# A conditioned decoder layer in fp32 on one core: folding of the pool weights, gate, first weight rows and LN powers rearranged

## The chip, the core and the metric

The kernel runs on one core of one Trainium2 chip. The core has TensorE (PE, with its weight loads PEld), VectorE (DVE), ScalarE (ACT), GpSimd (POOL) and SyncE (SP), and 16 DMA engines that move data between device memory and the core. The metric is the time of one execution on the device, in microseconds.

## The reference

A sequence of 4096 tokens with 1024 features goes through one layer: a layer norm that is scaled and shifted by a vector (adaLN), one input projection to 2560 columns, two mixers, one output projection, and a gated residual with a final layer norm.

```python
mod = silu(c) @ w_ada + b_ada                      # c: (1, 1024), w_ada: (1024, 3072)
shift, scale, gate = split(mod, 3)
h = layer_norm(x) * (1 + scale) + shift            # x: (1, 4096, 1024)
u_a, z_a, glu_b, z_b = split(h @ w_in + b_in, ...) # 512, 512, 1024, 512 columns
pooled = causal_multiscale_pool(u_a)               # 4 groups of 128; trailing mean minus token
y_a = (einsum("bsgc,gcd->bsgd", pooled, w_pool) + b_pool) * ls_pool * silu(z_a)
v = glu_b[..., :512] * sigmoid(glu_b[..., 512:])
v = silu(layer_norm(conv31(v) + b_dw) * ln_conv_g + ln_conv_b)
y_b = (v @ w_pw + b_pw) * silu(z_b)
y = concat(y_a, y_b) @ w_out + b_out
out = layer_norm(2 ** 0.25 * x + gate * y) * ln_post_g + ln_post_b
```

## The kernel before

**Products.** A product in fp32 accuracy is made of three matmuls on halves (mm3, L336 to L339): the high half of the weights times the high half of the activations (L337), the same weights times the low half (L338), and the low half of the weights times the high half of the activations (L339). High halves are written by ACT, low halves by DVE as the difference.

**Stages.** The tokens are worked on in 8 blocks (sb) of 512, in three phases over all blocks. In phase 1 a block is normed and modulated, and goes through 8 products of the gated linear unit (columns 8 to 15 of `w_in`, taken in pairs m and 4 + m: `p_<sb>_8` and `p_<sb>_12` are the first pair) and 2 products for z_a or z_b (`p1z`). Its activations x2 (in the rows `x_<sb>_<k>`, k = 0 to 7) are stored to device memory (xD), and its v too (vD). Phase 2 loads x2 again and makes 10 products a block, with pooling on DVE. The convolution runs on DVE (helpers that the rows show as L57x, 31 taps in pairs, on tiles cv, cx and ca), some of it beside phase 1, and its layer norm (conv_ln) lies between the phases' other work. Phase 3 makes the product with w_pw, the output projection and the final norm.

**The start.** The modulation vector is summed on DVE: mod_block (L173 to L192) multiplies eight tiles of w_ada, 128 rows each, by the entries of silu(c), and adds them up (L181), for five blocks of 1, 1, 2, 2 and 2 times 128 columns of scale and shift; a matmul with ones (L186) then sums over the partitions. Block 0's x is turned on TensorE (turn_x) and modulated from there by ACT (L321, L323) and DVE (mod_turned). The weights of phase 1 come as 8 rows of `w_in`, each 128 x 1024 in fp32 (load_row, L389, the tile in the order's rows is `wr`). split_cols cuts each row into high and low halves (L195, `wg0h` to `wg7h` and `wg0l` to `wg7l`), in two pieces: columns 0 to 2 and column 3 of each half of the row (a column here is 128 wide). Six products of block 0 run along with this, row by row; the seventh and eighth, which need column 3, and the z pair, follow when all rows are there.

**Later blocks.** row_stats loads the block's x in four tiles of 128 tokens, and col_stats (L263) takes of each a sum (ACT, L265), a negative mean (DVE), a sum of squares (ACT, L267), a variance (DVE, L268) and a power -0.5 (POOL, L269, one column). to_rows turns the eight columns on TensorE (`xcp`), stores them (rD), and they are loaded again, spread over all partitions (xbc). norm_T loads the transposed x (xk, L291), adds and multiplies (DVE, L292, L294), and mod_xT writes the halves (ACT L303, DVE L304). conv_ln does its statistics with the same col_stats, up to eight tiles a call (`ccp`).

**The fold.** fold_u (L350) multiplies the transposed weights of u_a by w_pool times ls_pool (wpl, made by DVE at L484), so that phase 2 gets the pooled mixer's product in one step. For each of four groups g it loads wT (L352), makes eight matmuls in two banks (L358, `fv`), copies each bank with ACT, stores the result (uD), and makes one matmul for the bias (L363, `bu`). In the code this stands behind block 0. mod_gate (L140) sums the gate's part of w_ada on DVE, and stands behind block 1.

**What sets the order.** The code is written block by block, but a scheduler reorders each engine's instructions by a timeline of its own, within the dependencies. Pools of rotating buffers limit it: 12 for x2, 6 for ca, 2 for cv, 2 for wraw (the raw weights, wT, the fold's result wf and the gate's tiles), 5 for tm (x, xk, xbc), and in PSUM 4 accumulation banks (acc), 2 for turning (tpb) and 2 others (s2b). Nearly all DMAs are issued by SP, in one order; the phase-2 loads of x2 are issued by POOL. The stores of block 0's x2 (L439) carry an explicit dependency on the last modulation sum.

## Time and profile before

| | |
|---|---|
| times of three runs | 1394.03, 1406.85, 1406.32 us (median 1406.32) |
| the profiled execution's own time | 1397.84 us |
| its span | 1395.8 us |
| mean granted clock of TensorE | 0.992 |
| TensorE busy | 97% of the span |
| DVE busy | 86% |
| ACT busy | 31% |
| POOL busy | 9% |
| moved by DMA | 243.81 MB, mean 175 GB/s |

The profile is of one execution, with times counted from the start of its span. In its rows stand the start, the duration or mean duration, the engine, the line of the kernel's text, the operation, and the tiles as out<-in. A bracket at a row's end gives the idle time of that engine just before, and what ended it. An engine runs its instructions in the order in which the program has them, so that one which waits holds up all behind it.

### The profile page before, as it was taken

Reading aid. Unit: us, or ns where it says so; the run is one execution under the profiler, and the core shown is the slowest. Engines: PE = TensorE matmul, PEld = TensorE weight load, DVE = VectorE, ACT = ScalarE, POOL = GpSimd, SP = SyncE. Lnnn points to the kernel's source line nnn. Section 1 sums busy time; section 2 is a strip of 40 time slices with the busy share of each in tenths; the row PEclk is TensorE's granted clock in tenths of the full one; section 3 lists DMA queues with packets and bytes.
Section 4 is the critical chain, followed back from the end, with each engine's and each line's share of the span. In section 5 each row is a group of like instructions: output and inputs, shape, how many; then the busy total and the mean of one; then the engine's idle time right before and its main releaser. Section 6 shows DMA issues by size and latency. Waiting matters only on the chain.

```text
span 1395.8 us, 17137 instructions
## 1 busy us (share of the span) xinstructions
PE 1356.4 (97%) x6045; PEld 1118.5 (80%) x6045; DVE 1193.9 (86%) x2348; ACT 432.6 (31%) x772; POOL 131.0 (9%) x193
## 2 busy tenths in 40 slices
PE   4898999999999999999999999999999999999997
PEld 3777888888888888888888888888888888888886
DVE  8688989983569999899899699999997899998754
...
GB/s 323 328 180 323 214 275 267 163 267 235 180 249 124 226 194 83 131 233 23 182 139 59 234 67 123 131 203 196 157 167 148 139 159 118 162 129 130 186 61 76
DMA packets 113352, 243.81 MB, mean 175 GB/s; under 512 B 15027, under 2 KB 45555, under 8 KB 113267
## 3 DMA queue, kind: packets, MB, share of 16 engines
...
q8 instruction: 47, 0.77, 0.2%
...
## 4 chain that ended last, share of the span: by engine, by line
PE 90%; DMA 5%; DVE 2%; ACT 2%; SPq 1%; issue 1%; DVEq 0%; ACTq 0%
PE po L713 25%; PE p L338 6%; PE p L339 6%; PE p L337 6%; PE p2z L338 4%; PE p2u L338 4%; PE p2z L337 4%; PE p2z L339 4%; PE p2u L337 4%; PE p2u L339 4%; PE pw L689 2%; PE pw L691 2%; PE pw L690 2%; PE p2b L338 2%; PE p2b L337 2%; PE p2b L339 2%
## 5 line engine op out<-in xcount | busy, mean ns | idle before, releaser
L576 DVE SCALAR_TENSOR_TENSOR cx<-cv,wdw,cx 128x513 f32<-128x513 f32 (+1 forms) x240 | 145.7, 613 | 0.7
L576 DVE SCALAR_TENSOR_TENSOR ca<-cx,wsum,ca 128x256 f32<-128x256 f32 (+1 forms) x240 | 143.7, 611 | 0.1
L576 DVE SCALAR_TENSOR_TENSOR ca<-cv,wdw,ca 128x256 f32<-128x256 f32 (+1 forms) x224 | 134.3, 611 | 0.0
L742 POOL TENSOR_TENSOR ors<-ove,mhalf 128x1 f32<-128x1 f32 x32 | 46.9, 1467 | 408.8 <-DVE ove L738 400.4
L736 ACT ACTIVATE ojk<-r,osm 128x1024 bf16<-128x1024 f32 x31 | 35.6, 1148 | 148.3 <-DVE osm L733 148.3
L332 POOL DMA_DIRECT2D x2r<-xD x64 | 34.8, 544 | 402.8 <-PE p2b L339 276.7
L731 DVE SCALAR_TENSOR_TENSOR r<-po,r 128x512 f32<-128x512 f32 x62 | 40.9, 687 | 22.0 <-PE po L713 21.9
L576 DVE SCALAR_TENSOR_TENSOR lx<-lv,wdw,lx 128x257 f32<-128x257 f32 x120 | 57.5, 479 | 0.0
L576 DVE SCALAR_TENSOR_TENSOR la<-lx,wsum,la 128x256 f32<-128x256 f32 x120 | 57.3, 478 | 0.0
L576 DVE SCALAR_TENSOR_TENSOR la<-lv,wdw,la 128x256 f32<-128x256 f32 x112 | 53.3, 478 | 0.0
L269 POOL TENSOR_TENSOR xcs<-smx,mhalf 128x1 f32<-128x1 f32 x28 | 20.7, 740 | 343.9 <-DVE smx L268 343.6
L517 ACT ACTIVATE sz<-p2z,cols 128x512 f32<-128x512 f32 x32 | 22.0, 688 | 95.6 <-PE p2z L339 95.5
L292 DVE TENSOR_TENSOR xk<-xk,xbc 128x1024 f32<-128x1024 f32 x28 | 34.1, 1222 | 17.2 <-DMA xk<-in_x_t_dram 17.2
L303 ACT ACTIVATE x<-xk,shc 128x512 fp32r<-128x512 f32 x56 | 38.0, 719 | 31.5 <-DVE xk L294 31.5
L304 DVE SCALAR_TENSOR_TENSOR x<-xk,shc,x 128x512 fp32r<-128x512 f32 x56 | 40.4, 749 | 8.3 <-ACT x L303 8.3
L524 ACT ACTIVATE u<-p2u,bu 128x512 f32<-128x512 f32 x32 | 22.0, 689 | 70.4 <-PE p2u L339 70.4
L745 DVE SCALAR_TENSOR_TENSOR r<-r,ors,b_bc 128x1024 f32<-128x1024 f32 (+1 forms) x33 | 41.1, 1248 | 3.2 <-POOL ors L742 3.1
L443 ACT ACTIVATE sg<-p,cols 128x512 f32<-128x512 f32 x32 | 21.9, 686 | 70.3 <-PE p L339 69.8
L265 ACT ACTIVATE x<-x 128x1024 f32<-128x1024 f32 x28 | 29.6, 1059 | 40.6 <-DMA x<-in_x_dram 39.7
L713 PE MATMUL po<-wo0h,ya 128*128 128x512 f32 x128 | 41.2, 392 | 0.0
L713 PE MATMUL po<-wo1h,ya 128*128 128x512 f32 x128 | 41.1, 390 | 0.0
L705 DVE SCALAR_TENSOR_TENSOR r<-r,gbo 128x1024 f32<-128x1024 f32 x32 | 39.0, 1218 | 1.7 <-DMA r<-in_x_dram 1.7
...
## 6 DMA issues: line engine op xcount, KB each, us to landing
...
```

Of the source, the lines that this page charges most:

```text
L303: nc.scalar.activation(h2[:, 0, :], z, AF.Identity, bias=shc[:, k : k + 1])
L304: nc.vector.scalar_tensor_tensor(h2[:, 1, :], z, shc[:, k : k + 1], h2[:, 0, :].bitcast(F32), op0=ALU.add, op1=ALU.subtract)
L337: nc.tensor.matmul(ps, w[0], X[0], start=first, stop=False)
L338: nc.tensor.matmul(ps, w[0], X[1], start=False, stop=False)
L339: nc.tensor.matmul(ps, w[1], X[0], start=False, stop=last)
L576: nc.vector.scalar_tensor_tensor(dst, src, wt, dst, op0=ALU.mult, op1=ALU.add)
L705: xg = nc.vector.scalar_tensor_tensor(r, r, ALPHA, gbo, op0=ALU.mult, op1=ALU.add)
L713: mm = nc.tensor.matmul(po[h], lhs, Wo[k][wi][:, h * 512 : (h + 1) * 512], start=(k == 0 and wi == 0 and lhs is yh), stop=last)
L731: nc.vector.scalar_tensor_tensor(r[:, sl], po[h], 1.0, r[:, sl], op0=ALU.mult, op1=ALU.add, accum_out=sm[:, h : h + 1])
L736: nc.scalar.activation(jk, r, AF.Square, bias=sm[:, 2:3], accum_out=ss)
L742: nc.gpsimd.tensor_tensor(rs, ve, mhalf[:, 0:1], op=ALU.pow)
L745: nc.vector.scalar_tensor_tensor(r[:, sl], r[:, sl], rs, b_bc[:, sl], op0=ALU.mult, op1=ALU.add)
```

## The change

Six things are changed.

1. *The fold.* Its four groups go to the ends of blocks 2, 3, 4 and 5. wT of a group is loaded a block earlier, its result wf has a tm buffer, and its banks are those for turning. wpl stands behind block 1 in the code.
2. *The gate.* mod_gate and its two matmuls go into phase 2, behind its third block (GATE_SB = 2).
3. *The first weight rows.* Each row is loaded with 768 of its 1024 columns (columns 0 to 2 of both halves). The remaining column 3 of both halves is loaded afterwards, by eight small loads in two tiles (`w3r`). The raw z weights (wzr) move from wraw to the buffers of gate and gbo.
4. *x of block 1.* Its four tiles are loaded among the first loads, into the ca buffers (x_early), and block 0's stores of x2 come behind the loads of xk for block 1.
5. *The modulation sums.* DVE sums six of the eight tiles; the last two are multiplied on TensorE, which adds them in the same accumulation: per column 3 matmuls in place of 1.
6. *The LN powers.* col_stats scales x by -1/n as it sums, so that the sum is the negative mean, and takes the scale back with -n ahead of the square; the two DVE steps per tile are gone. inv_root adds and takes the power on POOL once per block, on 4 or 8 columns together, and the constant left over goes into s1n and lcg.

The new lines of mod_block, of the statistics and of the fold, and the places where they are called (its other hunks are names and shapes):

```diff
-        for kt in range(KT):
+        nv = KT - 2
+        for kt in range(nv):
...
-                nc.tensor.matmul(ps[:, nk * i + j : nk * i + j + 1], acc[:, 1 - i, j * P : (j + 1) * P],
-                                 ones[:, 0:1], start=True, stop=True)
+                o = ps[:, nk * i + j : nk * i + j + 1]
+                sl = slice(j * P, (j + 1) * P)
+                nc.tensor.matmul(o, acc[:, 1 - i, sl], ones[:, 0:1], start=True, stop=False)
+                for kt in range(nv, KT):
+                    nc.tensor.matmul(o, wts[kt][:, 1 - i, sl], sc[:, kt : kt + 1], start=False, stop=kt == KT - 1)
...
-    def col_stats(src, n, nmean, rstd, name):
-        sm = st.tile([P, 3], F32, tag="sm", bufs=4, name=f"sm{name}")
-        nc.scalar.activation(src, src, AF.Identity, accum_out=sm[:, 0:1])
-        nc.vector.tensor_scalar(nmean, sm[:, 0:1], -1.0 / n, None, op0=ALU.mult)
-        nc.scalar.activation(src, src, AF.Square, bias=nmean, accum_out=sm[:, 1:2])
-        nc.vector.tensor_scalar(sm[:, 2:3], sm[:, 1:2], 1.0 / n, EPS, op0=ALU.mult, op1=ALU.add)
-        nc.gpsimd.tensor_tensor(rstd, sm[:, 2:3], mhalf[:, 0:1], op=ALU.pow)
+    def col_stats(src, n, nmean, ss):
+        nc.scalar.activation(src, src, AF.Identity, scale=-1.0 / n, accum_out=nmean)
+        nc.scalar.activation(src, src, AF.Square, bias=nmean, scale=-float(n), accum_out=ss)
+
+    def inv_root(ss, n):
+        nc.gpsimd.tensor_scalar(ss, ss, n * EPS, None, op0=ALU.add)
+        nc.gpsimd.tensor_tensor(ss, ss, mhalf[:, : ss.shape[1]], op=ALU.pow)
...
-            xt = load_x(i)
-            col_stats(xt, D, cs[:, t : t + 1], cs[:, 4 + t : 5 + t], f"x{i}")
+            xt = x_early[t] if sb == 1 else load_x(i)
+            col_stats(xt, D, cs[:, t : t + 1], cs[:, 4 + t : 5 + t])
+        inv_root(cs[:, 4:8], D)
...
-    def fold_u(g, wpl):
-        wT = wraw(f"wT{g}")
-        nc.sync.dma_start(wT, w_in_t[g * P : (g + 1) * P, :])
-        wf = wraw(f"wf{g}")
+    wTs = []
+
+    def fold_u(g, wpl, wT):
+        wf = ph.tile([P, D], F32, tag="tm", bufs=5, name=f"wf{g}")
...
-            pb = s2_bank(f"fv{g}_{hb}")
+            pb = tp_bank(f"fv{g}_{hb}")
...
-                   cst.tile([P, D], F32, tag=("gate", "gbo")[home - 2], name=f"wr{k}"))
-        nc.sync.dma_start(rows[k], w_in[k * P : (k + 1) * P, 8 * P : 16 * P])
+                   cst.tile([P, D], F32, tag=("gate", "gbo")[home - 2], name=f"wr{k}"))[:, : 6 * P].rearrange(
+                       "p (h c) -> p h c", h=2)
+        nc.sync.dma_start(rows[k], w_in[k * P : (k + 1) * P, 8 * P : 16 * P].rearrange(
+            "p (h c) -> p h c", h=2)[:, :, : 3 * P])
...
+    x_early = []
+    for t in range(TT):
+        xt = s2.tile([P, D], F32, tag="ca", bufs=6, name=f"x{TT + t}", padded_shape=[P, 2 * (HQ + T + 1)])
+        nc.sync.dma_start(xt, tok(xv, TT + t))
+        x_early.append(xt)
...
+        hi, lo = (both(t)[:, :, : 3 * P] for t in Wg[k])
+        nc.scalar.copy(hi, rows[k])
         xT.append(mod_turned(pb, k))
-        split_cols(k, 0, 3)
-        split_cols(k, 3, 4)
+        nc.vector.tensor_tensor(lo, rows[k], hi.bitcast(F32), op=ALU.subtract)
...
+    for q in range(2):
+        raw = wraw(f"w3r{q}").rearrange("p (k h c) -> p k h c", k=4, h=2)
+        for k in range(4):
+            nc.sync.dma_start(raw[:, k], both(w_in[(4 * q + k) * P : (4 * q + k + 1) * P, 8 * P : 16 * P])[:, :, 3 * P :])
+        for k in range(4):
+            hi, lo = (both(t)[:, :, 3 * P :] for t in Wg[4 * q + k])
+            split(hi, lo, raw[:, k])
...
+    nc.vector.tensor_scalar(s1n, s1, math.sqrt(D), None, op0=ALU.mult)
+    lcg = cst.tile([P, MC], F32, name="lcg")
+    nc.vector.tensor_scalar(lcg, vec("lncg", 0, MC), math.sqrt(DH), None, op0=ALU.mult)
...
+        if sb == 0:
+            for k in range(KT):
+                for i in range(2):
+                    after(nc.sync.dma_start(xD[k][0][:, i, :], xT[k][i].bitcast(F32)), x_loads[1])
...
-        if sb == 0:
+        if sb == 1:
...
-            for g in range(MC):
-                fold_u(g, wpl)
-        if sb == 1:
-            mod_gate(gbo)
...
+        if 1 <= sb <= MC:
+            wT = wraw(f"wT{sb - 1}")
+            nc.sync.dma_start(wT, w_in_t[(sb - 1) * P : sb * P, :])
+        if 2 <= sb <= MC + 1:
+            fold_u(sb - 2, wpl, wTs.pop(0))
+        if 1 <= sb <= MC:
+            wTs.append(wT)
...
+        if sb == GATE_SB:
+            mod_gate(gbo)
+            gb = wraw("gb")
+            nc.sync.dma_start(gb, b_ada[2 * D : 3 * D].partition_broadcast(P))
+            for h in range(2):
+                sl = slice(h * 512, (h + 1) * 512)
+                gp = tp_bank(f"gp{h}")
+                nc.tensor.matmul(gp, ones, gbo[:, sl], start=True, stop=True)
...
-            col_stats(pb, DH, cs[:, q : q + 1], cs[:, nq + q : nq + q + 1], f"c{s0}_{q}")
+            col_stats(pb, DH, cs[:, q : q + 1], cs[:, nq + q : nq + q + 1])
+        inv_root(cs[:, nq : 2 * nq], DH)
```

In the whole program TensorE has 5975 rows in place of 5946, DVE 2081 in place of 2223, POOL 139 in place of 173, SP 544 in place of 545, and ACT 625 as before.

On TensorE, at the end of block 0 and the start of block 1, the order of before is this (`fv` and `bu` are the fold's, `x_1_0` the first activations of block 1, `wg0h` and `wg0l` the halves of the first weight row; a number behind a name is the tile's):

```order
L358 MATMUL fv_1_1075<-wpl,wT_1066 128x128 x4
L363 MATMUL bu_1082<-cols,wpl 128x1
L337 MATMUL p_1_8_1192<-x_1_0_962,wg0h 128x512
L337 MATMUL p_1_12_1193<-x_1_0_962,wg0h 128x512
L337 MATMUL p_1_9_1247<-x_1_0_962,wg0h 128x512
L337 MATMUL p_1_13_1248<-x_1_0_962,wg0h 128x512
L358 MATMUL fv_0_1088<-wpl,wT_1085 128x128 x4
L358 MATMUL fv_1_1094<-wpl,wT_1085 128x128 x4
L363 MATMUL bu_1101<-cols,wpl 128x1
L358 MATMUL fv_0_1107<-wpl,wT_1104 128x128 x4
L358 MATMUL fv_1_1113<-wpl,wT_1104 128x128 x4
L338 MATMUL p_1_8_1192<-x_1_0_962,wg0h 128x512
```

In the changed order the same place, from the last matmul of block 0 on, reads:

```order
L348 MATMUL p1z_1_1038<-x_0_7_759,wz1l 128x512
L346 MATMUL p_1_8_1118<-x_1_0_968,wg0h 128x512
L346 MATMUL p_1_12_1119<-x_1_0_968,wg0h 128x512
L346 MATMUL p_1_9_1173<-x_1_0_968,wg0h 128x512
L346 MATMUL p_1_13_1174<-x_1_0_968,wg0h 128x512
L347 MATMUL p_1_8_1118<-x_1_0_968,wg0h 128x512
L348 MATMUL p_1_8_1118<-x_1_0_968,wg0l 128x512
L347 MATMUL p_1_12_1119<-x_1_0_968,wg0h 128x512
L348 MATMUL p_1_12_1119<-x_1_0_968,wg0l 128x512
```

The fold's eight rows are gone from here; the first of them now stand behind the last product of block 2. The first product of block 1 with the low half (L347, which was L338) stands fifth behind block 0's last matmul, where it was thirteenth (one row of the fold precedes the rows shown of before).

On ACT, in the start, the casts of the fifth to eighth weight row and the steps of x_0_4 stand like this before (`x_843` is a tile of block 1's x, whose statistics are L265 and L267; `hs_4` is a step of x_0_4):

```order
L195 CAST wg4h<-wr_409 128x2x384
L195 CAST wg4h<-wr_409 128x2x128
L195 CAST wg5h<-wr_411 128x2x384
L195 CAST wg5h<-wr_411 128x2x128
L265 ACTIVATE x_843,smx_845<-x_843 128x1024
L195 CAST wg6h<-wr_421 128x2x384
L195 CAST wg6h<-wr_421 128x2x128
L321 ACTIVATE x_0_4_628<-xt_4_605,shc,s_281 128x512
L267 ACTIVATE x_843,smx_845<-x_843,xcs_842 128x1024
L195 CAST wg7h<-wr_423 128x2x384
L195 CAST wg7h<-wr_423 128x2x128
L323 ACTIVATE hs_4_630<-x_0_4_628,shn 128x512
```

And in the changed order (L270 and L271 are now the statistics, on the four tiles x_426 to x_432; L430 the cast of 768 columns, and L200 that of column 3):

```order
L430 CAST wg5h<-wr_412 128x2x384
L330 ACTIVATE x_0_4_646<-xt_4_622,shc,s_281 128x512
L270 ACTIVATE x_428,xcs_870<-x_428 128x1024
L332 ACTIVATE hs_4_648<-x_0_4_646,shn 128x512
L270 ACTIVATE x_430,xcs_870<-x_430 128x1024
L271 ACTIVATE x_428,xcs_870<-x_428,xcs_870 128x1024
L430 CAST wg6h<-wr_422 128x2x384
L271 ACTIVATE x_430,xcs_870<-x_430,xcs_870 128x1024
L430 CAST wg7h<-wr_424 128x2x384
L270 ACTIVATE x_432,xcs_870<-x_432 128x1024
L200 CAST wg0h<-w3r_783 128x2x128
L330 ACTIVATE x_0_5_676<-xt_5_652,shc,s_281 128x512
```

The sums of all four tiles of block 1 and the squares of three have moved ahead of x_0_5's first step, and so has a cast of column 3, while the second cast of each weight row is gone from its place; the other seven casts of column 3 and the last square follow ahead of x_0_5's second step.

On SP, the DMA issues around the load of wpl are these before (`cv` is the convolution's load of v, `rD` and `xbc` are the store of block 1's statistics and their load):

```order
L482 DMA wpl<-in_w_pool_dram 128x4x128
L439 DMA xD_0_157<-x_0_7_741 128x512
L446 DMA vD_0_165<-v_0_894 128x512
L565 DMA cv_0_6444<-vD_0_165 128x2x256
L446 DMA vD_0_173<-v_1_899 128x512
L446 DMA vD_0_181<-v_2_904 128x512
L565 DMA cv_1_6501<-vD_0_173 128x2x256
L276 DMA rD_270<-rowsx_877 8x128
L286 DMA xbc_880<-rD_270 128x1024
L291 DMA xk_0_882<-in_x_t_dram 128x2x512
L291 DMA xk_2_887<-in_x_t_dram 128x2x512
L291 DMA xk_4_978<-in_x_t_dram 128x2x512
```

And in the changed order:

```order
L510 DMA wpl<-in_w_pool_dram 128x4x128
L516 DMA wT_1798<-in_w_in_t_dram 128x1024
L467 DMA vD_0_165<-v_0_900 128x512
L467 DMA vD_0_173<-v_1_905 128x512
L282 DMA rD_270<-rowsx_883 8x128
L598 DMA cv_0_6382<-vD_0_165 128x2x256
L598 DMA cv_1_6439<-vD_0_173 128x2x256
L293 DMA xbc_886<-rD_270 128x1024
L300 DMA xk_0_888<-in_x_t_dram 128x2x512
L300 DMA xk_2_893<-in_x_t_dram 128x2x512
L467 DMA vD_0_181<-v_2_910 128x512
L300 DMA xk_4_984<-in_x_t_dram 128x2x512
```

The stores of block 0's x2 (xD_0) are gone from here, and stand behind the last load of xk. wpl and two loads of wT stand ahead of the store of v and of the statistics.

More of the change, by code (lines that the diff above doesn't have):

```diff
@@ L34 @@
 EARLY = 2
+GATE_SB = 2
 PERSB = (1, 1, 1, 1, 1, 1, 0, 0)
@@ L66, in tile_layer @@
     nc.vector.memset(ones, 1.0)
-    mhalf = cst.tile([P, 4], F32, name="mhalf")
+    mhalf = cst.tile([P, 2 * TT], F32, name="mhalf")
     nc.vector.memset(mhalf, -0.5)
@@ L391, in load_row, with both @@
         rows[k] = (wraw(f"wr{k}") if home < 2 else
-                   cst.tile([P, D], F32, tag=("gate", "gbo")[home - 2], name=f"wr{k}"))
-        nc.sync.dma_start(rows[k], w_in[k * P : (k + 1) * P, 8 * P : 16 * P])
+                   cst.tile([P, D], F32, tag=("gate", "gbo")[home - 2], name=f"wr{k}"))[:, : 6 * P].rearrange(
+                       "p (h c) -> p h c", h=2)
+        nc.sync.dma_start(rows[k], w_in[k * P : (k + 1) * P, 8 * P : 16 * P].rearrange(
+            "p (h c) -> p h c", h=2)[:, :, : 3 * P])
+    def both(t):
+        return t.rearrange("p (h c) -> p h c", h=2)
     mods = ((0, 1), (1, 1), (2, 2), (4, 2), (6, 2))
@@ L400, in tile_layer @@
             load_row(k)
-    def split_cols(k, m0, m1):
-        split(*(t.rearrange("p (h c) -> p h c", h=2)[:, :, m0 * P : m1 * P] for t in (*Wg[k], rows[k])))
+    x_early = []
[3 more added lines that the diff above has]
+        x_early.append(xt)
     xT = []
@@ L424, in tile_layer @@
     for q in range(2):
-        raw = wraw(f"wzr{q}")
+        raw = cst.tile([P, D], F32, tag=("gate", "gbo")[q], name=f"wzr{q}")
         nc.sync.dma_start(raw.rearrange("p (k n) -> p k n", k=4),
@@ L436, in tile_layer @@
     gbo = cst.tile([P, D], F32, tag="gbo", name="gbo")
-    for k in range(KT):
-        for i in range(2):
-            after(nc.sync.dma_start(xD[k][0][:, i, :], xT[k][i].bitcast(F32)), last, True)
     def glu(sb, m, pa, pg):
@@ L485, in tile_layer @@
             nc.vector.tensor_tensor(bpl, vec("b_pool", 0, 4), vec("ls", 0, 4), op=ALU.mult)
-            for g in range(MC):
-                fold_u(g, wpl)
-        if sb == 1:
-            mod_gate(gbo)
-            gb = wraw("gb")
-            nc.sync.dma_start(gb, b_ada[2 * D : 3 * D].partition_broadcast(P))
-            for h in range(2):
-                sl = slice(h * 512, (h + 1) * 512)
-                gp = tp_bank(f"gp{h}")
-                nc.tensor.matmul(gp, ones, gbo[:, sl], start=True, stop=True)
-                nc.vector.tensor_tensor(gate_bc[:, sl], gp, gb[:, sl], op=ALU.add)
-            nc.sync.dma_start(gbo, b_out.partition_broadcast(P))
-            nc.vector.tensor_tensor(gbo, gbo, gate_bc, op=ALU.mult)
+        if 1 <= sb <= MC:
[5 more added lines that the diff above has]
+            wTs.append(wT)
     ph_ctx.close()
@@ L554, in tile_layer @@
             nc.sync.dma_start(zD[1][sb][:, m - 2, :], sz)
+        if sb == GATE_SB:
[6 more added lines that the diff above has]
+                nc.tensor.matmul(gp, ones, gbo[:, sl], start=True, stop=True)
+                nc.vector.tensor_tensor(gate_bc[:, sl], gp, gb[:, sl], op=ALU.add)
+            nc.sync.dma_start(gbo, b_out.partition_broadcast(P))
+            nc.vector.tensor_tensor(gbo, gbo, gate_bc, op=ALU.mult)
     ph_ctx.close()
```

10 lines of the change are left out of this document (6 added, 4 removed).

## The prediction

> **What bounds the kernel now.** I read the page first, then the table of engines by stretch, then TensorE in order of time where that table shows it short of work.
>
> ```profile
> PE 1356.4 (97%) x6045; PEld 1118.5 (80%) x6045; DVE 1193.9 (86%) x2348; ACT 432.6 (31%) x772; POOL 131.0 (9%) x193
> ...
> 0.00:35.00 35.00, 14.86 (x57) 11.77 (x58) 28.16 (x75) 13.93 (x19) 4.16 (x37) 0.97 1.00 323
> 35.00:70.00 35.00, 30.96 (x150) 25.13 (x149) 21.09 (x45) 19.20 (x31) 1.10 (x2) 0.98 0.97 328
> 70.00:105.00 35.00, 31.65 (x145) 26.33 (x144) 31.09 (x70) 15.07 (x28) 1.62 (x2) 0.90 0.55 178
> 105.00:140.00 35.00, 31.58 (x144) 26.95 (x145) 29.77 (x77) 16.23 (x29) 2.89 (x4) 0.90 0.88 322
> ...
> 560.00:700.00 140.00, 140.00 (x634) 115.96 (x633) 129.09 (x220) 28.78 (x70) 15.54 (x24) 1.00 0.40 137
> ```
>
> The columns are the stretch, its length, then busy time of PE, PEld, DVE, ACT and POOL, the granted clock, the DMA share and GB/s. TensorE bounds the kernel: of the 39.4 us in which it is idle, 20.1 + 4.0 + 3.4 + 3.4 lie in the first 140 us, and in 560 to 700 it has none. So only what happens before 140 us can shorten the program; work that leaves DVE, ACT or POOL later is worth nothing by itself. Within those 140 us there is one hole, at 95 to 115:
>
> ```profile
> 95.00:100.00 5.00, 2.72 (x11) 1.75 (x10) 5.00 (x9) 2.21 (x5) 0.00 (x0) 0.75 0.84 239
> 100.00:105.00 5.00, 3.93 (x18) 3.85 (x18) 5.00 (x11) 3.17 (x7) 0.00 (x0) 0.56 0.14 30
> 105.00:110.00 5.00, 1.58 (x7) 1.61 (x8) 5.00 (x11) 0.63 (x2) 0.00 (x0) 0.78 0.87 314
> 110.00:115.00 5.00, 5.00 (x19) 4.37 (x18) 4.72 (x10) 3.27 (x5) 0.00 (x0) 0.54 0.91 280
> ...
> 80.42 0.27 PE L73 MATMUL xcp<-ident,xcs 128*8 128x128 f32 x1
> ...
> 93.50 1.95 PE L358 MATMUL fv<-wpl,wT 128*128 128x128 f32 x16
> ...
> 97.62 2.07 PE L337 MATMUL p<-x,wg0h 128*128 128x512 f32 x4 [2.01 <-ACT x L303]
> 99.96 3.75 PE L358 MATMUL fv<-wpl,wT 128*128 128x128 f32 x16 [0.27 <-DMA wT<-in_w_in_t_dram]
> ...
> 108.42 3.76 PE L358 MATMUL fv<-wpl,wT 128*128 128x128 f32 x16 [4.49 <-DMA wT<-in_w_in_t_dram]
> 111.83 0.77 PE L338 MATMUL p<-x,wg0h 128*128 128x512 f32 x1
> ```
>
> TensorE works in order. It finishes block 0 at 93.50, and the second matmul of block 1 (L338) starts only at 111.83: three folds stand before it, two of them waited for a load, and the granted clock fell to about half, so a fold that took 1.95 us takes 3.75.
>
> **The change, part by part.** *The fold.* All four folds leave this place. L338 of block 1 then waits for the later of two things: TensorE's end of block 0, and the low half of x_1_0 from DVE. The latter was written here:
>
> ```profile
> 72.59 0.69 DVE L484 TENSOR_TENSOR wpl<-wpl,lsb 128x512 f32<-128x512 f32 x1
> ...
> 77.48 0.44 DVE L570 TENSOR_TENSOR cx<-cv 128x271 f32<-128x271 f32 x1 [1.62 <-DMA cv<-vD]
> ...
> 78.11 0.34 DVE L574 TENSOR_SCALAR ca<-cv,wdw 128x256 f32<-128x256 f32 x1
> 78.37 0.35 DVE L574 TENSOR_SCALAR ca<-cx,wsum 128x256 f32<-128x256 f32 x1
> ...
> 79.03 0.48 DVE L576 SCALAR_TENSOR_TENSOR ca<-cv,wdw,ca 128x256 f32<-128x256 f32 x1
> 79.42 0.48 DVE L576 SCALAR_TENSOR_TENSOR ca<-cx,wsum,ca 128x256 f32<-128x256 f32 x1
> ...
> 94.91 1.23 DVE L292 TENSOR_TENSOR xk<-xk,xbc 128x1024 f32<-128x1024 f32 x1
> 96.05 1.42 DVE L294 SCALAR_TENSOR_TENSOR xk<-xk,s,xbc 128x512 f32<-128x512 f32 x2
> 97.37 0.49 DVE L576 SCALAR_TENSOR_TENSOR ca<-cv,wdw,ca 128x256 f32<-128x256 f32 x1
> ...
> 103.93 0.76 DVE L304 SCALAR_TENSOR_TENSOR x<-xk,shc,x 128x512 fp32r<-128x512 f32 x1
> ...
> 67.30 0.38 SPq L482 DMA_DIRECT2D wpl<-in_w_pool_dram  x1
> ...
> 82.62 2.06 SPq L291 DMA_DIRECT2D xk<-in_x_t_dram  x4
> ```
>
> From start to start a tap costs 0.39 us, a first tap 0.26, an L292 1.14, a pair of L294 1.32. In the changed order 2 sums (0.36 each), 6 first taps, 21 taps, 4 of L292, 2 pairs of L294 and one L445 (0.67) stand from the first conv instruction to that low half, and its own 0.7 ends it: 0.7 + 1.6 + 8.2 + 4.6 + 2.6 + 0.7 + 0.7 = 19.1 us. The transposed sums (xcp) stand about 10 us earlier, ahead of p_0_11, but SP issues their store behind the wpl load, the second wT load (which waits for wpl's product on DVE, 5.3 us after wpl's issue) and two stores of v. Block 0 starts its tail about 1.4 us earlier (below), so wpl goes at 66, its product at 71.3, xk's loads at about 76 instead of 82.62, and the first conv instruction at about 77 as before. I take 77 + 19.1 = 96.1 for L338. If the loads come in time and DVE is not late the bound is TensorE itself, 92.1; if the start loses what I expect it to gain, and a load is late, 100.
>
> L338 is thus 111.83 - 96.1 = 15.7 us earlier. Three folds must still be paid, warm, at the 1.95 us of the row at 93.50 and a little for bu: -6.1. Behind 111.83 the matmuls ran at a clock of 0.54 for the 3.2 us to 115, which gives +1.6. Net 11.2 us, from 7 (at 100) to 15 (at 92.1). The folds in blocks 2 to 5 have wT loaded a block ahead, so their loads are covered; ACT empties their banks while the second half is multiplied. (A block has 240 matmuls; at 634 in 140 us that is 53 us.) The 16 stores of x_0 now wait on SP until the last xk load has landed, and behind them stand the stores of v, z and x_1 and the loads of block 2's x; these are wanted a block later, so I count 0, and a microsecond for a microsecond should they come late.
>
> *The modulation sums.* They take 16 sums off DVE and put 32 matmuls of one column on TensorE.
>
> ```profile
> L181 DVE SCALAR_TENSOR_TENSOR macc<-wa,sc,macc 128x512 f32<-128x512 f32 x21 | 15.3, 747 | 0.1
> L181 DVE SCALAR_TENSOR_TENSOR macc<-wa,sc,macc 128x256 f32<-128x256 f32 x14 | 6.8, 483 | 0.3
> ...
> 43.68 0.95 PE L186 MATMUL mod<-ones,macc 128*128 128x1 f32 x8
> 44.48 0.63 PE L73 MATMUL xt<-ident,x 128*128 128x128 f32 x4
> ```
>
> Off DVE go 6 x 0.75 and 4 x 0.48 (two per block of modulation): 6.4 us of DVE time, ahead of which TensorE waited. Eight records, four matmuls, take 0.80 us, so 32 more cost 6.4 us of TensorE, in a stretch where it is idle 24 us. By these rows the two sums cancel only where TensorE waits for nothing else; I count the lead as 0 for the first weight row, where the mod matmuls run cold and now stand ahead of all of its products, and as some 3 us by the fourth.
>
> *Weight rows and the early x.* Rows of 768 columns save 8 x 128 KB, but three of the four loads of x for block 1 now come ahead of the last rows, so these land as before. What they add is ACT work just there:
>
> ```profile
> 41.42 1.14 ACT L195 CAST wg4h<-wr 128x768 fp32r<-128x768 f32 x2 [1.48 <-DMA wr<-in_w_in_dram]
> ...
> 47.04 1.06 ACT L265 ACTIVATE x<-x 128x1024 f32<-128x1024 f32 x1 [2.94 <-DMA x<-in_x_dram]
> 48.00 0.19 ACT L265 ACTIVATION_READ_ACCUMULATOR x<-x 128x1 f32 x1
> ...
> 50.02 1.14 ACT L267 ACTIVATE x<-x,xcs 128x1024 f32<-128x1024 f32 x1
> 51.06 0.19 ACT L267 ACTIVATION_READ_ACCUMULATOR x<-x,xcs 128x1 f32 x1
> ...
> 59.50 0.48 PE L338 MATMUL p<-x,wg5h 128*128 128x512 f32 x1
> ```
>
> ACT has four statistics (2.4 us each, 9.5), four casts of 768 and eight of 256 (0.7 and 0.3 each, the pair at 41.42 split by its columns), and the three steps of x_0_4 and x_0_5 (2.2, at two thirds of the L267 row's 1.14 for half its columns) in a row from about 40, where the first early x lands (1.4 us ahead of the row at 41.42): 17.1 us. The last of them ends at 57, and the low half of x_0_5 is there at about 58.4 after one DVE step, where the old one let L338 start at 59.50. The 3 us of lead thus shrink to 1 to 1.5; bounds +3 and -5 by when the eight small loads of columns 3 land. This is inside the 96.1.
>
> *The rest.* The gate's ten or so DVE microseconds go to phase 2, where DVE has 10.9 us of slack in 140 and the result is needed only in phase 3: 0. The powers and 120 single-column DVE steps lie beside TensorE: 0, as long as xcp and ccp are not late (third rival). The final tail is untouched.
>
> [...]
>
> **The rivals.** (1) *No hole at all*: DVE and loads keep up, L338 at 92 or the start gains its 3 us: 15 to 18 us, 1397.84 - 16.5 = 1381. For it: the xk loads meet less traffic, since the 16 stores of x_0 now wait for them. Against: the taps ahead of x_1_0. (2) *The start pays*: ACT's queue and the w3 loads hold x_0_5 for 4 us more than the old order did, and block 1 slips with it: 11.2 - 5 = 6 us, 1392. For it: DVE has all eight low halves of columns 3 and both of wz ahead of x_0_5 and x_0_6. (3) *Slower: the powers on POOL.*
>
> ```profile
> L269 POOL TENSOR_TENSOR ccs<-smc,mhalf 128x1 f32<-128x1 f32 x32 | 24.3, 767 | 95.6 <-DVE smc L268 95.0
> L269 POOL TENSOR_TENSOR xcs<-smx,mhalf 128x1 f32<-128x1 f32 x28 | 20.7, 740 | 343.9 <-DVE smx L268 343.6
> ```
>
> No row shows a power of 4 or 8 columns. Should it cost by the column, 4 x 0.74 and 8 x 0.77 come after the last sum where one came: +2.2 and +5.4 us, plus the added sum (0.7). TensorE would stand at xcp and ccp wherever they were placed for less: if none of this is covered, 7 x 2.9 + 4 x 2.9 + 2 x 6.1 = 44 us, 1431; it turns the sign from about a quarter of it on. The other bound is a cost by the instruction, where nothing is late. I take the latter, since ACT had to wait for xcp on TensorE and not the reverse, so there is slack. [...] (4) *Nothing moves*: the folds meet new waits in their blocks worth what they cost here.
>
> **How the numbers follow.** The forecast against the profiled execution: 1397.84 - 11.2 = 1386.6. That execution lies low among the four that are known (1394.03, 1397.84, 1406.32, 1406.85); their middle is 1402.1, the stated median 1406.32 (8.5 over the profiled one), and nothing in the profile says which level the changed kernel meets. So 1402.1 - 11.2 = 1391, and I take 1390. Chances: forecast 0.55, no hole 0.15, the start pays 0.17, powers 0.07, nothing 0.06. Low end: 1394 less 16.5, 1377; high end: 1406 less 5, 1402; both ends of the unknown terms and three of the other cases fall inside. A difference of 1% (14 us) is about what a measurement of this kernel tells from none; faster by that means under 1392.3. The forecast does it in six of ten, no hole in nine of ten, the start in two of ten: 0.33 + 0.13 + 0.03 = 0.49. Slower by 1% comes only from the powers and a little of the rest, 0.07.
>
> **What would show it.** L347 of block 1 (the old L338) at 94 to 98 us, at full clock or nearly; no idle before the folds' matmuls; TensorE idle 2 to 5 us between 48 and 60; nothing idle behind 120; ACT without a pause from 40 to 57. Wrong if block 1 starts behind 100, if xcp or ccp get a wait for POOL, or if gp waits for DVE.

## The result, and the profile after

The changed kernel takes 1420.96 us (median of four runs, 1417.60 to 1421.26), against 1401.23 us before (four runs, 1394.03 to 1406.85): ratio 1.0129, 95% interval 1.0083 to 1.0176. The kernel before took 1393 to 1400 us in some executions and 1403 to 1409 in others, for a reason that no run shows, and the share of the longer ones differs between the batches of the experiments (6 of 19, 0 of 14, 15 of 21 and 2 of 19), so that a ratio can shift by up to 0.7% on that account alone. The changed kernel is slower by 1.3%, where 1390 was forecast. The profiled execution has a span of 1419.4 us, against 1395.8 before.

The first row of the changed kernel's page, and its table of engines by stretch (stretch, length, busy time of PE, PEld, DVE, ACT and POOL, granted clock, DMA share, GB/s):

```profile
PE 1371.0 (97%) x6109; PEld 1129.2 (80%) x6109; DVE 1178.4 (83%) x2220; ACT 432.5 (30%) x772; POOL 115.5 (8%) x159
...
35.00:70.00 35.00, 35.00 (x175) 29.48 (x174) 18.30 (x40) 23.25 (x40) 1.27 (x2) 0.90 0.72 228
70.00:105.00 35.00, 31.49 (x127) 25.07 (x126) 28.91 (x59) 10.88 (x16) 0.00 (x0) 0.90 0.90 311
105.00:140.00 35.00, 35.00 (x156) 28.89 (x155) 31.31 (x73) 12.95 (x21) 1.58 (x2) 1.00 0.65 243
140.00:280.00 140.00, 133.91 (x606) 110.25 (x606) 124.98 (x233) 59.24 (x99) 14.24 (x6) 0.98 0.54 194
280.00:420.00 140.00, 140.00 (x639) 116.06 (x638) 50.68 (x68) 57.16 (x94) 3.79 (x6) 1.00 0.59 212
...
840.00:980.00 140.00, 126.88 (x551) 102.86 (x550) 138.16 (x296) 36.16 (x67) 4.40 (x7) 0.94 0.45 151
980.00:1120.00 140.00, 137.61 (x604) 112.36 (x603) 126.36 (x256) 49.02 (x90) 14.13 (x11) 0.99 0.45 154
```

The hole of the first 140 us has closed as forecast, but TensorE is now idle 6.1 us in 140 to 280 and 13.1 us in 840 to 980, where before it was not idle at all. Its waits, grouped (us in all, times, longest), name the places:

```profile
PE mod L190 <- DVE macc L183: 10.0, 2, 8.9
PE po L747 <- ACT ya L200: 9.1, 2, 8.6
PE ccp L74 <- POOL ccs L275: 6.1, 2, 4.5
...
PE pw L723 <- ACT vp L200: 2.3, 1, 2.3
...
PE xcp L74 <- POOL xcs L275: 1.6, 1, 1.6
```

How far the changed kernel is behind (+) the kernel before, by the silu that follows each block's last z product (phase 1), by the last of phase 2, and at the end of the span:

| end of | before | after | difference |
|---|---|---|---|
| block 0 | 93.70 | 96.81 | +3.1 |
| block 1 | 170.04 | 155.49 | -14.6 |
| block 2 | 226.37 | 210.53 | -15.8 |
| block 3 | 284.30 | 277.45 | -6.9 |
| block 6 | 447.45 | 447.63 | +0.2 |
| phase 2 | 946.70 | 947.67 | +1.0 |
| program | 1395.8 | 1419.4 | +23.6 |

Block 0's +3.1 is not TensorE's: its last matmul of that block starts at 93.51 where it started at 93.26, but the silu stands on ACT behind a step that waits for DVE. So a lead of 16 us was won at the start, given back in blocks 3 to 6, and another 22.6 us were lost in phase 3. Three places have to be read.

**Block 1.** TensorE's timeline, as the prediction asked for it:

```profile
97.53 0.63 PE L346 MATMUL p<-x,wg0h 128*128 128x512 f32 x1 [2.96 <-ACT sgz L479]
98.72 0.80 PE L347 MATMUL p<-x,wg0h 128*128 128x512 f32 x1 [0.55 <-DVE x L313]
```

L347 starts at 98.72, where L338 started at 111.83. The wait of 2.96 us ahead of it ended, by the profile, with the silu of block 0's last z product (`sgz`, at 96.81), which stood on ACT behind a step of block 1's x that had waited for DVE.

**Block 3.** The timeline of POOL, then of DVE, then of TensorE:

```profile
233.52 4.50 POOL L274 TENSOR_SCALAR xcs<-xcs 128x4 f32<-128x4 f32 x1 [60.34 <-ACT x L271]
238.11 1.04 POOL L275 TENSOR_TENSOR xcs<-xcs,mhalf 128x4 f32<-128x4 f32 x1
239.13 6.19 POOL L274 TENSOR_SCALAR ccs<-ccs 128x4 f32<-128x4 f32 x1
...
300.31 0.23 POOL L274 TENSOR_SCALAR xcs<-xcs 128x4 f32<-128x4 f32 x1 [53.88 <-ACT x L271]
...
237.86 0.75 DVE L466 SCALAR_TENSOR_TENSOR v<-p,cols,sg 128x512 f32<-128x512 f32 x1
...
244.48 0.75 DVE L609 SCALAR_TENSOR_TENSOR ca<-cx,wsum,ca 128x512 f32<-128x512 f32 x1
246.94 1.23 DVE L301 TENSOR_TENSOR xk<-xk,xbc 128x1024 f32<-128x1024 f32 x1 [1.71 <-DMA xk<-in_x_t_dram]
...
239.20 0.27 PE L74 MATMUL xcp<-ident,xcs 128*8 128x128 f32 x1 [1.58 <-POOL xcs L275]
246.49 0.38 PE L74 MATMUL ccp<-ident,ccs 128*8 128x128 f32 x1 [4.50 <-POOL ccs L275]
```

An addition on four columns, 0.23 us at 300, takes 4.50 and 6.19 us here. The first ends when DVE begins an instruction that reads v's product from PSUM (237.86), the second when DVE has nothing to do (244.48 + 0.75 = 245.23); until then DVE ran one tap behind the other. TensorE waits for both, and its next matmuls, to 251, are 0.43 us apart at a granted clock of 0.50, where they were 0.23 us apart at 240.

**The start of phase 3.** TensorE, and DVE's L640, the step with which a convolution norm begins:

```profile
953.40 0.38 PE L74 MATMUL ccp<-ident,ccs 128*8 128x128 f32 x1 [1.64 <-POOL ccs L275]
...
964.93 1.22 PE L747 MATMUL po<-wo0h,ya 128*128 128x512 f32 x2 [8.62 <-ACT ya L200]
...
421.88 2.49 DVE L640 TENSOR_TENSOR ca<-ca,cbc 128x512 f32<-128x512 f32 x4 [0.26 <-DMA cbc<-cD]
630.03 4.63 DVE L640 TENSOR_TENSOR ca<-ca,cbc 128x1024 f32<-128x1024 f32 x4 [0.47 <-DMA cbc<-cD]
...
958.43 2.50 DVE L640 TENSOR_TENSOR ca<-ca,cbc 128x512 f32<-128x512 f32 x4 [0.36 <-DMA cbc<-cD]
```

And the same steps of the kernel before:

```profile
400.08 2.50 DVE L606 TENSOR_TENSOR ca<-ca,cbc 128x512 f32<-128x512 f32 x4 [8.56 <-DMA cbc<-cD]
596.17 4.63 DVE L606 TENSOR_TENSOR ca<-ca,cbc 128x1024 f32<-128x1024 f32 x4 [3.64 <-DMA cbc<-cD]
...
918.96 2.49 DVE L606 TENSOR_TENSOR ca<-ca,cbc 128x512 f32<-128x512 f32 x4
```

The last norm of the convolution's main part came 27.7 us ahead of the end of phase 2, and now comes 10.8 us behind it, in the middle of the first work of phase 3. TensorE's 8.62 us hang on it by a buffer. The spread rows of the norm (`cbc`) and phase 3's load of the pooled mixer's result (`ya`) share one more pool, of two buffers (tag `bc` in the code), so the load of ya goes out when L640 has ended, at 958.43 + 2.50 = 960.93, and ACT and TensorE wait for it. The changed kernel's two rows, then the load in the kernel before, behind its own L606 (918.96 + 2.49 = 921.45) but 30.5 us ahead of the first matmul that uses it (952.02):

```profile
960.95 0.32 SPq L710 DMA_DIRECT2D ya<-yD  x1
964.26 1.14 ACT L200 CAST ya<-ya 128x512 fp32r<-128x512 f32 x2 [2.53 <-DMA ya<-yD]
...
921.48 0.32 SPq L676 DMA_DIRECT2D ya<-yD  x1
```

In e1 and e13 the load goes out within 0.04 us of L640's end as well (927.79 and 939.31). The lateness, 39.5 us at this norm, builds up earlier: it was 21.8 us at the first norm, and 33.9 at the second. Why the first is late is seen in the changed kernel's SP and ACT:

```profile
391.94 2.28 SPq L266 DMA_DIRECT2D x<-in_x_dram  x3
394.32 0.38 SPq L370 DMA_DIRECT2D uD<-wf  x1
394.74 1.42 SPq L266 DMA_DIRECT2D x<-in_x_dram  x1
...
412.98 0.26 ACT L281 COPY rowsx<-xcp 8x128 f32<-8x128 f32 x1 [3.31 <-PE xcp L74]
413.14 0.25 ACT L281 COPY rowsc<-ccp 8x128 f32<-8x128 f32 x1
```

The x of block 7 is loaded at 392 to 396, around the store of the last fold's result wf, where the kernel before loaded it at 356 to 365. Its statistics come with it, and the rows of the first convolution norm (`rowsc`) stand behind the rows of block 7 (`rowsx`) on ACT, although TensorE had turned them at 246.49. DVE cannot go on with the convolution before that norm has released its buffers, so it has 50.68 us of work in 280 to 420 where it had 79.16.

### The profile page after: what moved, and what is told of

It reads as the page before. It is cut to its first block, busy times and chain, and to the rows that moved or that the text cites. A ratio compares the mean times of both kernels' runs of the same rounds, so it can differ in the third digit from the quotient of the medians.

```text
span 1419.4 us, 17051 instructions
## 1 busy us (share of the span) xinstructions
PE 1371.0 (97%) x6109; PEld 1129.2 (80%) x6109; DVE 1178.4 (83%) x2220; ACT 432.5 (30%) x772; POOL 115.5 (8%) x159
## 4 chain that ended last, share of the span: by engine, by line
PE 88%; DVE 5%; DMA 3%; ACT 1%; POOL 1%; SPq 1%; issue 1%; DVEq 0%; ACTq 0%; POOLq 0%
PE po L747 24%; PE p L346 7%; PE p L347 7%; PE p L348 7%; PE p2u L347 4%; PE p2z L347 4%; PE p2z L348 4%; PE p2u L348 4%; PE p2u L346 4%; PE p2z L346 4%; PE p2b L348 2%; PE p2b L347 2%; PE p2b L346 2%; PE pw L723 2%; PE pw L725 2%; PE pw L724 2%
## 5 line engine op out<-in xcount | busy, mean ns | idle before, releaser
L609 DVE SCALAR_TENSOR_TENSOR cx<-cv,wdw,cx 128x257 f32<-128x257 f32 (+1 forms) x240 | 145.0, 611 | 1.2
L466 DVE SCALAR_TENSOR_TENSOR v<-p,cols,sg 128x512 f32<-128x512 f32 x32 | 23.8, 745 | 71.9 <-ACT sg L464 68.9
L539 ACT ACTIVATE sz<-p2z,cols 128x512 f32<-128x512 f32 x32 | 22.0, 688 | 121.8 <-PE p2z L348 113.1
L301 DVE TENSOR_TENSOR xk<-xk,xbc 128x1024 f32<-128x1024 f32 x28 | 34.1, 1218 | 21.8 <-DMA xk<-in_x_t_dram 17.7
L200 ACT CAST yb<-z 128x512 fp32r<-128x512 f32 x32 | 19.8, 617 | 81.1 <-DVE z L730 66.4
L747 PE MATMUL po<-wo2h,ya 128*128 128x512 f32 x128 | 40.0, 390 | 0.4 <-ACT ya L200 0.4
```

The lines of the kernel that those rows point to most:

```text
L609: nc.vector.scalar_tensor_tensor(dst, src, wt, dst, op0=ALU.mult, op1=ALU.add)
L747: mm = nc.tensor.matmul(po[h], lhs, Wo[k][wi][:, h * 512 : (h + 1) * 512], start=(k == 0 and wi == 0 and lhs is yh), stop=last)
```

## The experiments

Theory A: the hole at phase 3 is the convolution's chain on DVE, made late by wf in the tm pool and by the gate. Rivals stand with each run. Ratios are to the kernel before, run on the same chip in the same batch: its median was 1401.23 beside the changed kernel, 1397.24 beside e1 to e4, 1395.60 beside e5 to e8, 1405.32 beside e9 to e12 and 1396.96 beside e13 and e14. The last two columns are from the profiles: L640 (or L606) of the last main norm against the end of phase 2 (minus is ahead), and the time from the end of phase 2 to the end of the span.

| run | median us | ratio (95%) | last norm | phase 3 |
|---|---|---|---|---|
| before | 1401.23 | 1 | -27.7 | 449.1 |
| after | 1420.96 | 1.0129 (1.0083-1.0176) | +10.8 | 471.7 |
| e1 wf elsewhere | 1399.28 | 1.0003 (0.9976-1.0030) | -18.6 | 454.3 |
| e2 gate back | 1392.07 | 0.9948 (0.9923-0.9972) | -13.1 | 451.8 |
| e3 own rows | 1409.98 | 1.0100 (1.0053-1.0148) | -124.6 | 447.4 |
| e4 addition on DVE | 1415.30 | 1.0125 (1.0093-1.0158) | +13.4 | 474.3 |
| e5 two-input addition | 1419.55 | 1.0177 (1.0160-1.0194) | +10.8 | 472.4 |
| e6 fold alone | 1422.14 | 1.0194 (1.0179-1.0209) | +9.2 | 470.7 |
| e7 powers alone | 1400.54 | 1.0037 (1.0022-1.0052) | -40.2 | 449.0 |
| e8 e2 and e4 | 1398.36 | 1.0014 (1.0002-1.0026) | -10.3 | 455.1 |
| e9 e2, sums on DVE | 1389.86 | 0.9915 (0.9875-0.9955) | -12.4 | 453.1 |
| e10 e2, x late | 1417.30 | 1.0097 (1.0063-1.0132) | -12.8 | 452.4 |
| e11 e1, gate in block 6 | 1398.97 | 0.9969 (0.9947-0.9991) | -18.4 | 454.3 |
| e12 e11, e3 and e4 | 1392.79 | 0.9921 (0.9896-0.9945) | -113.1 | 447.4 |
| e13 gate left out | 1405.18 | 1.0053 (1.0032-1.0074) | -12.0 | 454.8 |
| e14 gate back, own rows, sums and addition on DVE | 1398.53 | 1.0008 (0.9986-1.0029) | -129.2 | 447.6 |

Where the last norm is 9 us or more behind, phase 3 takes 471 to 474 us; 10 to 19 us ahead, 452 to 455; 28 us or more ahead, 447 to 449. No run departs from this.

**e1**: the fold's result out of the tm pool (gate_bc and gbo are allocated behind phase 1 for it).

```diff
-        wf = ph.tile([P, D], F32, tag="tm", bufs=5, name=f"wf{g}")
+        wf = cst.tile([P, D], F32, tag=("gate", "gbo")[g % 2], name=f"wf{g}")
```

> The changed kernel, with the fold's result wf in the buffers of gate and gbo (free in phase 1) and not in the tm pool. Theory A (the convolution's chain on DVE is late: wf stands in the tm pool ahead of the next block's x, so the statistics of block 7 and with them the first convolution norm come some 20 us later, and the last one ends behind phase 2): the first norm's L640 at about 400 instead of 421.9, the idle time at 948 to 985 gone for the most part, 1398 to 1407 us against 1421. Rival B (phase 3 is late by itself, through the output weights and the loads of its first block): the idle time stays, 1421.

1399.28. The first norm is at 400.71. 17.4 us of the gain lie in phase 3, the rest ahead of it: in e1's order TensorE has no wait for ccp in block 3. Theory A holds, rival B falls.

**e2**: the block under `if sb == GATE_SB` moves back into phase 1, under `if sb == 1`.

> The changed kernel, with the gate's sums behind block 1 again. Theory A: some 13 us of DVE leave the convolution's chain in phase 2, the last convolution norm ends ahead of phase 3, the idle time at 948 to 985 shrinks by 10 to 20 us: 1400 to 1411. Rival B: 1421, or a little less by the two matmuls of the gate that now lie elsewhere.

1392.07, better than expected, in part because the new order also meets no wait for ccp in block 3, which e4 below prices at 8.5 us. Here the first norm (412.14) and the second (604.71) are 192.6 us apart, in the changed kernel 208.2. That confounds two things, so the gate was tried again in e11 and e13.

**e3**: a buffer of their own for the rows of the convolution norm.

```diff
-        rows = st.tile([n, P], F32, tag="rows8", bufs=2, name=f"rows{name}", padded_shape=[4 * TT, P])
+        own = name[0] == "c"
+        rows = st.tile([n, P], F32, tag="rowsc" if own else "rows8", bufs=1, name=f"rows{name}",
+                       padded_shape=[4 * TT, P])
```

> The changed kernel, with a buffer of their own for the convolution norm's rows (rows8 has one buffer in place of two, and the convolution norm another), so that the first convolution norm need not wait for the rows of block 7's statistics. Theory A: the first norm's L640 at 250 to 300 instead of 421.9, DVE idle some 50 us less between 280 and 420, the last norm some 100 us earlier, no idle time at the start of phase 3: 1421 - 22.6 = 1398. Rival B: 1421.

The first norm is at 258.28, DVE works 132.28 us of the stretch from 280 to 420 (50.68 in the changed kernel), and phase 3 has no hole (447.4): so the buffer order is what tied the convolution to block 7. But the time is 1409.98, 12 more than expected. With DVE full of taps, TensorE waits for POOL at two more places:

```profile
PE xcp L74 <- POOL xcs L275: 7.2, 3, 3.1
PE ccp L74 <- POOL ccs L275: 4.5, 1, 4.5
...
PE p2z L348 <- ACT sg L466: 1.6, 1, 1.6
PE p2u L348 <- DVE v L468: 1.4, 1, 1.4
```

These are e3's waits of TensorE; at the end of phase 2 it is 13.2 us behind the kernel before. In phase 1 the waits for POOL come to 11.7 us (6.1 in the changed kernel), and those for sg and v, where phase 1 turns into phase 2, to 3.0 (none there); that is 8.6 us more, and the rest of the 12 was not separated.

**e4**: `nc.gpsimd.tensor_scalar(ss, ss, n * EPS, ...)` becomes `nc.vector.tensor_scalar(...)`.

> The changed kernel, with the addition ahead of the power on DVE in place of POOL (one instruction a block). In the changed kernel the two additions on POOL in block 3 took 4.50 and 6.19 us, and TensorE waited 1.58 + 4.50 us and then ran at half clock. Theory A (the convolution's chain sets the time from phase 2 on): the waits at 239 and 246 go, blocks 3 to 7 are some 8 us earlier, but the chain on DVE is not, and the hole at phase 3 grows by about as much: 1419 to 1421. Rival C (losses add up): 1412.

Block 3 ends at 268.98 in place of 277.45: the two waits and the clock of 0.50 behind them were worth 8.5 us. Of these 5.9 reach the end of the profiled span. The expectation was off by about as much: the first norm is tied to block 7's rows, so the chain started earlier too (412.93), and phase 3 grew by only 2.6.

**e5**: the same addition on POOL with two inputs, at the same place in POOL's order.

```diff
-        nc.gpsimd.tensor_scalar(ss, ss, n * EPS, None, op0=ALU.add)
+        nc.gpsimd.tensor_tensor(ss, ss, epst[:, 0 if n == D else 1, : ss.shape[1]], op=ALU.add)
```

> The changed kernel, with the addition ahead of the power still on POOL and at the same place in every engine's order, but as an instruction with two inputs (a column of constants) in place of one input and an immediate. In the changed kernel the one-input addition took 4.50 and 6.19 us in block 3 while DVE ran one tap behind the other, 0.23 us elsewhere, and the two-input power behind it 1.04 us. Theory A (this form is held up by DVE's taps, the two-input form is not): both additions take about 1 us, TensorE's waits at 239 and 246 go, blocks 4 to 7 are some 8 us earlier, the whole as in the run with the addition on DVE: about 1415. Rival D (whatever comes first on POOL is held up there): additions of 4 to 6 us again, 1421.

The two-input form is held as long (POOL of e5):

```profile
230.73 4.50 POOL L277 TENSOR_TENSOR xcs<-xcs,epst 128x4 f32<-128x4 f32 x1 [59.68 <-ACT x L274]
...
236.28 6.24 POOL L277 TENSOR_TENSOR ccs<-ccs,epst 128x4 f32<-128x4 f32 x1
```

Rival D is right: it is not the form.

**e6**: the fold's hunks alone, on the kernel before.

> The kernel before, with the spread of the fold alone (blocks 2 to 5, wT a block earlier, wf in the tm pool, banks for turning). Theory A: block 1 starts some 12 us earlier, the folds give back some 8, and since wf stands ahead of the next block's x the first convolution norm is late again (L606 at about 415 to 425 against 400), the last one ends behind phase 2, and TensorE waits some 15 to 20 us there: 1397 - 5 + 18 = 1410, in any case slower than before. Rival E (the spread is a gain, and only the gate and the powers cost): 1397 - 10 = 1387.

1422.14: the spread alone costs as much as the whole change. Its waits at block 1 show that it does not even win the start:

```profile
102.13 2.07 PE L337 MATMUL p<-x,wg0h 128*128 128x512 f32 x4 [8.30 <-ACT x L303]
110.06 0.80 PE L338 MATMUL p<-x,wg0h 128*128 128x512 f32 x1 [5.86 <-DVE x L304]
```

L338 comes 1.8 us earlier than before, not 13, for x_1_0 isn't there; and the first norm is at 437.01. Phase 3 is 21.6 us longer, for a wait of 13.6 us for ya among others. Rival E falls; theory A's 1410 was 12 too low, since it counted on the early start.

**e7**: the hunks of the powers alone, on the kernel before.

> The kernel before, with the LN powers once per block alone (addition and power on POOL). Theory A: where the additions meet DVE's taps they take 4 to 6 us, TensorE waits at one or two of the turned sums, 2 to 9 us in phase 1, and nothing in phase 3: 1399 to 1406. Rival F (nothing is late, 140 single-column steps leave DVE): 1397 or less.

1400.54, 0.4% slower than the kernel before in its batch (1395.60). The number lies in theory A's range, but not by its mechanism: the additions took at most 0.94 us, not 4 to 6, and only one xcp waits for POOL (1.0 us). Whether the 0.4% is the powers' is open, for it is less than the batches of the kernel before differ by.

**e8**: e2 with the addition on DVE.

> The changed kernel, with the gate's sums behind block 1 again and the addition ahead of the power on DVE. Both theories of the parts: 1392 less the wait for the turned sums that was left there (1.9 us) and a little for the convolution's chain: 1388 to 1391, faster than the kernel before.

1398.36, slower than e2. TensorE waits 4.0 us for the first low halves of blocks 1 and 2 and 3.4 us for z from DVE in phase 3. Which of the reordered DVE instructions does it was not separated.

**e9**: e2 with `nv = KT`, so that all eight tiles are summed on DVE.

> The kernel of the run with the gate back behind block 1 (1392 us), with all eight modulation sums on DVE again. By the prediction's terms 6.4 us of DVE and 6.4 us of TensorE cancel: 1390 to 1394. Rival G (in the start DVE is what TensorE waits for, so sums on TensorE pay): TensorE waits longer in the first 60 us and block 1 starts 3 to 6 us later: 1395 to 1398.

1389.86, the fastest, and faster than the kernel before by 0.85% in its batch (whose median for that kernel is 1405.32; against the other batches' 1395.60 to 1397.24 it is 0.4 to 0.5%). Block 0 ends 2.9 us earlier than in e2, and L347 of block 1 starts at 92.94 in place of 96.03: so the 32 matmuls and the relief of DVE together cost 3 us on TensorE's path. Rival G falls. The stretch from 35 to 70, of e2 and then of e9, shows where:

```profile
35.00:70.00 35.00, 35.00 (x175) 29.35 (x174) 18.59 (x40) 23.27 (x41) 1.28 (x2) 0.90 0.71 225
...
35.00:70.00 35.00, 32.48 (x157) 25.74 (x156) 22.12 (x47) 25.23 (x45) 1.27 (x2) 1.00 0.71 228
```

TensorE of e2 has no pause, but its granted clock is 0.90, a loss of some 3.4 us: it was 0.50 from 44.4 to 47.8 and from 58.1 to 61.5, each time just behind a run of modulation matmuls of one column (24 records at 40.92 and at 54.28, 2.73 us each; a third such run, at 29.12, was not followed by it). With 8 such records in their place (0.95 us) e9 keeps a clock of 1.00. The matmuls themselves fill pauses: TensorE is busy 54.84 us of the first 70 in e2, and 46.95 in e9.

**e10**: e2 without x_early (the tiles come by load_x), and with the stores of x_0 where they stood.

> The kernel of the run with the gate back behind block 1 (1392 us), with x of block 1 loaded through the tm pool as before and the stores of x_0 ahead of the loads of xk. Theory H (the early x and the late stores are what let block 1 start when block 0 ends; with the fold's spread alone TensorE waited 14.2 us there): 8 to 12 us of waiting for x_1_0 at the start of block 1, 1400 to 1404. Rival G (the relief of DVE and the powers do it): 1392 to 1395.

1417.30. TensorE waits 7.0 + 6.0 us for x_1_0, L347 is at 109.65, and 7.8 us of waits for POOL are back in phase 1. Theory H holds: L347 is 13.6 us later than in e2, where 8 to 12 were expected. The rest of the 25 us by which the run is slower lies behind it, with those waits for POOL among it, and phase 3 is as long as in e2 (452.4). Early loads and late stores were not tried apart.

**e11**: e1, with the gate's block under `if sb == 6` in phase 1.

> The changed kernel, with wf in the buffers of gate and gbo and the gate's sums behind block 6, where DVE had some 60 us idle. Theory A (nothing but a late convolution chain costs time from phase 2 on): the chain is late neither by wf nor by the gate, no wait at the start of phase 3, 1390 to 1395. Rival B (the rest of the loss belongs to phase 3 or to the folds): 1399 as with wf moved alone.

1398.97, no better than e1. The gate's sums ran at 392.95 to 440.17, while the first norm is at 399.95: they still lay between the first and the second norm, which are 201.8 us apart (198.8 in e1). So this run did not take the gate off the chain, and says nothing against theory A; its number is rival B's.

**e12**: e11 with e3's buffer and e4's addition.

> The same, with rows of their own for the convolution's norm and the addition ahead of the powers on DVE: the waits for POOL (7.2 + 4.5 us in the run with own rows alone) cannot come, and the convolution runs early. Theory A and the reading of POOL: 1387 to 1391, the fastest. Rival I (in the run with own rows the rest of the loss, some 12 us where phase 1 turns into phase 2, came from a DVE that runs taps when v and x are due): 1396 to 1402.

1392.79. No wait for POOL is left, and phase 3 has no hole (447.4), but phase 2 ends only 2.5 us ahead of the kernel before, where e2 was 8.9 ahead. The time lies between the two ranges, and what it lacks was not separated.

**e13**: the changed kernel with `nc.vector.memset(gbo, 0.01)` in place of mod_gate.

> The changed kernel without the gate's eight loads and eight sums (gbo is filled with a constant; that part of the computation is left out). TensorE's order is the same through phase 1, so the first norm's L640 stays at about 422 and block 3's waits for POOL stay. If the gate's sums are a share of the lateness (they cost DVE 10 to 13 us between the first and the second norm): the second norm at 614 to 620 instead of 630, the hole at the start of phase 3 smaller by 10 to 16 us, 1405 to 1411. If the gate's place costs nothing (with wf moved, the gate in phase 2 and behind block 6 gave the same 1399): 1420.

1405.18, 15.8 us less. The rows of DVE's L640 in e13:

```profile
421.45 2.50 DVE L640 TENSOR_TENSOR ca<-ca,cbc 128x512 f32<-128x512 f32 x4 [0.42 <-DMA cbc<-cD]
614.50 4.63 DVE L640 TENSOR_TENSOR ca<-ca,cbc 128x1024 f32<-128x1024 f32 x4 [2.37 <-DMA cbc<-cD]
...
936.78 2.50 DVE L640 TENSOR_TENSOR ca<-ca,cbc 128x512 f32<-128x512 f32 x4 [0.24 <-DMA cbc<-cD]
```

The first norm is where it was, the second 15.5 us earlier, the last 21.7. So the gate has a share of its own. Its loads are left out with its sums; the sums alone are 9.8 us of DVE (513.8 to 546.1 in the changed kernel), and what makes 15 of them was not separated.

**e14**: the changed kernel with e2, e3, e4 and e9 together.

> The changed kernel with the gate behind block 1, rows of their own for the convolution's norm, the addition on DVE and all modulation sums on DVE: what each of the runs before showed as a gain, in one. If the gains add up: 1390 (gate back, sums on DVE) less the rest of the hole at phase 3 (about 2 us): 1386 to 1390. If the early convolution takes DVE where phase 1 turns into phase 2, as with own rows alone: 1392 to 1396.

1398.53: the gains don't add up. The profile is of the slowest of the ten executions (1404.75), so it shows more than the median lost. In it TensorE waits 7.2 us for the first low halves of blocks 1, 2 and 5, and 4.1 us for sg and v where phase 1 turns into phase 2, and phase 2 ends 8.7 us behind the kernel before. The 4.1 us are what the second theory said, an early convolution on DVE where phase 1 needs it; the waits at blocks 1 and 2 lie ahead of the first norm (269.23), and their cause is open.

## Why the prediction was wrong

**The fold at block 1** (L338 at 96.1, 15.7 us earlier): right within its bounds. It was at 98.72, 13.1 us earlier; the chain from the first convolution instruction took 19.5 us where 19.1 was summed, and began at 79.18 instead of 77. Behind the 2.96 us of waiting ahead of it the granted clock was 0.50 from 98 to 104, and matmuls were 0.43 us apart in place of 0.23 for 7 us, which is some 3 us of work; the prediction's sum had nothing for it. But the gain is not the fold's alone: without the early x it is gone (e6, e10).

**Folds repaid** (1.95 us and a little each): right in size, the rows at 210.33 and after show 1.95 + 0.28. "ACT empties their banks", "their loads are covered": right as well. What was not asked is where wf is put. It took a place in the tm ring ahead of the next block's x. This is the step that failed first: the text followed the fold's loads and banks, and not the buffer of its result. Taken out, it gave 21.7 us (e1), 17.4 of them in phase 3.

**The gate** (0, since DVE has 10.9 us of slack in 140 and the result is needed only in phase 3): failed. The slack was read from TensorE's and DVE's busy shares in phase 2. DVE's own chain had to reach its last norm before phase 3, whose first load of ya takes the norm's buffer, and had 27.7 us to spare there; the gate's 10 or so us of sums became 15 us between the first and the second norm (208.2 against 193.1), and 15.8 us of the time (e13). wf and the gate overlap: either one removed brings the chain back ahead of phase 3. "Nothing idle behind 120" and "only what happens before 140 us can shorten the program" come from the same step: true of gains, and taken for losses too.

**The powers** (0; third rival by the column): the mechanism that the rival feared, TensorE standing at xcp and ccp, came in one block, for 8.5 us (e4). The price by the column was not it: a power of 4 columns takes 1.04 us, of 8 columns 1.67 to 1.85, and one of 1 column 0.55 at 322.82 in the kernel before, with DVE idle. What took long was the addition ahead of it (4.50 and 6.19 us), a term that the prediction put at 0.7 us in the rival and at nothing in the sum. With these waits for POOL one of its own signs of being wrong had come.

**The modulation sums** (6.4 against 6.4 us, cancel): too good by 3 us (e9). Of the mod matmuls that the prediction calls cold, four records took 1.01 us at 15.71 in the kernel before, where eight took 0.95 at 43.68. The 6.4 us of DVE are ten sums, not the sixteen that the text names. TensorE has no idle time from 35 to 70 in the changed kernel, where 2 to 5 us were forecast between 48 and 60, and the term had no half clock behind the matmuls: 0.90 over that stretch, in the changed kernel as in e2. So TensorE ended block 0 0.25 us later than before, and not 1.4 earlier.

**The sum**: -15.8 us at the end of block 2 (the terms give -19.5 there, before any fold is repaid: 15.7, 1.6 and some 2.2 for the fourth fold, which ran at 121.88 in the kernel before and which the prediction left out on both sides), +8.9 for four folds and +8.5 for the waits at POOL make +1.6 by the terms; +0.2 was measured. Phase 2 adds 0.8, phase 3 22.6. A range that ended at 1402 held no case with a late convolution, though the page of the profile had DVE at 86%.
